# The first two weight panels of a hybrid decoder step multiplied together, k tile by k tile, with the sums of squares and the first rotation rearranged

## The chip, the cores and the metric

The kernel runs on one core of a Trainium2 chip. The metric is the device time of one execution in microseconds (us). Five engines of the core run beside each other, each taking its own instructions strictly in the order in which they were written: TensorE (matmuls; PE in the profile, PEld for its weight loads), VectorE (DVE), ScalarE (ACT), GpSimd (POOL) and SyncE (SP, which here only issues transfers). Waits between engines are by semaphores. Matmuls write to PSUM, and VectorE and ScalarE read results from there.

## What is computed

One layer of a decoder for 512 prompt tokens and 8 sample tokens together (520 columns), all float32. The stage that matters here is the beginning:

```python
u = rmsnorm(x, g_norm1)                       # x * rsqrt(mean(x^2) + eps) * g
qa, ka, va, qb, kb, vb, glr, rb, ga, gb = split(u @ w_in)
qa = rope(qa, pos); ka = rope(ka, pos)        # [x1*cos - x2*sin, x2*cos + x1*sin]
...                                           # windowed attention A, gated linear attention B, mix, MLP
```

The key buffers, value buffers and states of both groups are outputs too.

## The kernel before

**Layout.** Everything is kept transposed: 128 features on the partitions, the 520 tokens in the free dimension, as two halves of 260 columns. The model width of 1024 is eight k tiles. A *panel* is 128 output columns of a weight matrix with its eight k tiles, 512 KB. The panels are numbered in the order of use: 0 and 1 are the two halves (x1 and x2 of the rotation) of the first group's k, 2 and 3 those of its q, 4 and 5 its v, 6 and 7 the k of the second group, 8 and 9 its q, and so on to the MLP.

**A product in three passes.** To keep float32 accuracy, the activations and weights are each split into a high and a low part: `uh` and `ul` (lines 218 and 219), `whi` and `wlo` (lines 90 and 91, four k tiles at a time). ScalarE makes the high part, VectorE subtracts it from the original to get the low one. For each k tile TensorE then does high x high, low x high and high x low, each on two halves: six matmuls, so 48 for one panel (line 124). The names in the profile say which: `mps<-uh,whi`, `mps<-ul,whi`, `mps<-uh,wlo`.

**The norm comes late.** `uh` and `ul` hold x times g, not normalised. The sum of squares of each token runs beside the first panels (`stats`, line 230): eight squares on ScalarE, seven additions on VectorE, a matmul with ones that sums over the partitions (line 242), and an inverse root (`rsqrt`, lines 184 to 189) that gives `rb`. It is multiplied in later: the first pair, panels 0 and 1, is rotated with the plain cos and sin tables and scaled at the end (line 289); then `rb` is multiplied into the tables (line 848), and every later rotation comes out scaled.

**The rotation** (`rope_pair`, line 271). Panel A times cos and times sin (lines 276, 277), panel B times sin and times cos (280, 281), one subtraction and one addition of these `rt` tiles into `ro` (284, two instructions each), and eight transfers by SP that bring the result into `KTt` or `QTt` (291).

**The buffers that set the order.** Raw panels have two buffers, so the load of panel n+2 waits for the splitting of panel n. `whi` and `wlo` have four buffers each, of half a panel: the first half of panel n+2 can be split when TensorE is through the first half of panel n, the second half when TensorE is through with panel n. PSUM has two tiles for products (`pm`), and one more that panel 2 alone uses (`ps`): panel 3 takes panel 0's tile, panel 4 that of panel 1, panel 5 that of panel 3, and each has to wait until VectorE has read it.

**Who sets the order.** The kernel is written as a sequential program, and a scheduler puts each engine's instructions in an order by a model of their times; instructions written under `high_priority` go before others that are ready. `panel_mms` splits the next panel in this way (line 114). What stands in a queue when an engine waits stays behind the wait.

**The beginning** (`start`, line 197). SP issues k tile 0 of x, panel 0 in two halves, the other k tiles of x, panel 1, then the tables and panel 2. TensorE runs 20 matmuls on ones meanwhile (`keep_warm`), then panel 0, panel 1, panel 2 and so on, one after the other.

Of the kernel before, what the change touches and what calls it, by code (L numbers as in the profile page):

```python
# [21 lines left out]
P = 128  # L22
HC = 260
# [17 lines left out]
def halves(t):  # L41
    return t.rearrange("p (j c) -> p j c", j=2)


class Build:
# [24 lines left out]
    def load_panel(self, i, parts=1):  # L70
        src, kt = self.panels[i]
        raw = self.rawp.tile([P, kt, P], F32, tag="raw", name="raw", bufs=self.rawb)
        for x in range(parts):
            ks = slice(x * kt // parts, (x + 1) * kt // parts)
            self.nc.sync.dma_start(raw[:, ks], src[:, ks])
        self.raw[i] = raw

    def split_panel(self, i):

        nc = self.nc  # L80
        src, kt = self.panels[i]
        raw = self.raw.pop(i)
        self.split[i] = out = []
        for x in range(0, kt, 4):
            n = min(4, kt - x)
            if i in self.wdst:
                hi, lo = (t[:, x:x + n] for t in self.wdst[i])
            else:
                hi, lo = (self.wp.tile([P, n, P], F32R, tag=t, name=t, bufs=self.wbufs) for t in ("whi", "wlo"))
            nc.scalar.activation(hi, raw[:, x:x + n], AF.Copy)  # L90
            nc.vector.tensor_tensor(lo, raw[:, x:x + n], hi.bitcast(F32), op=ALU.subtract)  # L91
            out.append((hi, lo))
# [13 lines left out]
    def panel_mms(self, xh, xl, m, pool=None):  # L106


        nc, i = self.nc, self.cur
        self.cur += 1  # L110
        if i + 2 < len(self.panels):
            self.load_panel(i + 2)
        if i + 1 < len(self.panels):
            with self.tc.high_priority():
                self.split_panel(i + 1)
        wt = self.split.pop(i)
        kt = KT // m
        for c in range(m):
            ps = [] if c % 2 else (pool or self.pm).tile([P, 2, 512], F32, tag="m", name="mps")
            out = [self.bank("mps")[:, :HC] if c % 2 else ps[:, j, :HC] for j in range(2)]  # L120
            for k in range(kt):
                for n, (w, x) in enumerate(self.passes(wt, c * kt + k, xh, xl)):
                    for j in range(2):
                        self.last = nc.tensor.matmul(  # L124
                            out[j], w, x[:, k, j * HC:(j + 1) * HC],
                            start=(k == 0 and n == 0), stop=(k == kt - 1 and n == 2))
                self.emit_tiny(self.tiny_rate)
            yield out if c % 2 else ps[:, :, :HC]
# [68 lines left out]
    def start(self):  # L197
# [15 lines left out]
        self.keep_warm(20)  # L213
        self.eps = self.cp.tile([P, 1], F32, tag="eps", name="eps")
        nc.vector.memset(self.eps, EPS)
        nc.scalar.preload_act_table_set("natural_log_exp_and_others")
        for k in range(KT):
            self.split_x = nc.scalar.activation(self.uh[:, k], xr[:, k], AF.Copy, scale=self.g("n1", k))
            nc.vector.scalar_tensor_tensor(self.ul[:, k], xr[:, k], self.g("n1", k), self.uh[:, k].bitcast(F32),  # L219
                                           op0=ALU.mult, op1=ALU.subtract)  # L220
            if k == 0:
                self.split_panel(0)
        return xr
# [6 lines left out]
    def stats(self, ap, xr):  # L230
# [3 lines left out]
        for k in range(KT):  # L234
            a = ap.tile([P, NT], F32, tag="sq", name="sq", bufs=6)
            self.after(nc.scalar.activation(a, xr[:, k], AF.Square), self.split_x)
            if acc is None:
                acc = a
            else:
                nc.vector.tensor_tensor(acc, acc, a, op=ALU.add)  # L240
# [13 lines left out]
    def rope_tables(self):  # L254
# [5 lines left out]
        return self.cs, self.sn  # L260
# [10 lines left out]
    def rope_pair(self, dst, gi, psA, mmB, late=None):  # L271
# [4 lines left out]
        nc.vector.tensor_tensor(V[0], psA, cs, op=ALU.mult)  # L276
# [5 lines left out]
        for x, (a, b, op) in enumerate(((0, 2, ALU.subtract), (3, 1, ALU.add))):  # L282
            o = self.rp.tile([P, NT], F32, tag="ro", name="ro", bufs=3)
            self.cols(o, gi > 0, lambda ov, sel: nc.vector.tensor_tensor(ov, sel(V[a]), sel(V[b]), op=op))
            if late and x == 0:
                late()
            if late:
                rbv = halves(self.rb)
                self.cols(o, False, lambda ov, sel: nc.vector.tensor_tensor(ov, ov, sel(rbv), op=ALU.mult))
# [8 lines left out]
    def proj_qk(self, gi, late=None):  # L298
        nc, O = self.nc, self.O
        for dst, out in ((self.KTt, O["kT"]), (self.QTt, None)):  # L300
            self.rope_pair(dst, gi, self.mm(), self.mm, late)
            late = None
# [494 lines left out]
    def run(self):  # L797
# [30 lines left out]
        xr = self.start()  # L828
# [9 lines left out]
        rp, aps, gps, gss = (ExitStack() for _ in range(4))  # L838
        right = dict(bufs=1, side="right")
        self.rp = rp.enter_context(tc.tile_pool(name="rp", **right))  # L840
        with ps_stack:
            cs = self.rope_tables()

            def late():
                with tc.tile_pool(name="stp", **right) as p:
                    self.stats(p, xr)
                for t in cs:
                    nc.vector.tensor_tensor(t, t, self.rb, op=ALU.mult)

            self.late_consts()  # L850
            self.proj_qk(0, late)
# [333 lines left out]
```

## Time and profile before

| | |
|---|---|
| median of three timed runs | 938.59 us (937.89 to 943.15) |
| the profiled execution | 939.2 us |
| its span, first to last instruction | 937.4 us |
| TensorE busy | 920.3 us, 98% |
| VectorE busy | 549.0 us, 59% |
| ScalarE busy | 380.0 us, 41% |
| TensorE's mean granted clock | 0.993 |
| moved by DMA | 155.27 MB, 166 GB/s on average |

Busy time is the time in which an engine has an instruction in work; matmuls overlap, so 98% doesn't say that TensorE does as much as it could, only that it is seldom without work. Times in a profile count from the first instruction. In a timeline a row has the start, the time, the engine, the line of the kernel, the operation, the tile written and those read, the shape, and in brackets how long the engine had been idle before it and for whom it waited. The granted clock is the share of full speed at which TensorE was allowed to run.

### The profile page before, as it was taken

The numbers are of one execution on the slowest core, as the hardware profiler recorded it, in microseconds if no ns is written. First come the engines' busy times: TensorE is split into PE (matmuls) and PEld (weight loads), VectorE is DVE, ScalarE is ACT, GpSimd is POOL, SyncE is SP. The second block draws the span as 40 slices with busy tenths as digits, with TensorE's granted clock in tenths as the row PEclk, the third lists the DMA queues.
The fourth block names the chain that finished last, engine by engine and source line by source line (L and its number), as shares of the span: only waits on it lengthen the run. The fifth ranks groups of instructions, "written<-read, shape, count | busy, mean of one in ns | idle before, by whom it ended". The sixth has DMA issues, their size and how long they took to land.

```text
span 937.4 us, 19831 instructions
## 1 busy us (share of the span) xinstructions
PE 920.3 (98%) x8306; PEld 896.3 (96%) x8306; DVE 549.0 (59%) x1078; ACT 380.0 (41%) x735; POOL 67.4 (7%) x119
## 2 busy tenths in 40 slices
PE   9899999999999999999999999999999999999995
PEld 9899999999998999989999999999999999999995
DVE  7757566665766949586855556433443345555654
ACT  6133423443645536565633443322432243224432
POOL 1000000000201112010000000010000000000000
PEclk9899999999999999999999999999999999999998
DMA  6365454233444444222677767777865232323301
GB/s 245 114 237 181 142 191 155 101 131 116 166 150 165 128 165 144 69 74 69 235 278 277 272 226 269 270 269 270 294 254 175 96 93 87 104 92 106 121 30 63
DMA packets 37147, 155.27 MB, mean 166 GB/s; under 512 B 5129, under 2 KB 11537, under 8 KB 35106
## 3 DMA queue, kind: packets, MB, share of 16 engines
q1 hardware_dynamic: 32066, 95.26, 29.8%
q0 software_dynamic: 4848, 58.73, 18.0%
q8 instruction: 65, 1.06, 0.5%
q14 instruction: 24, 0.20, 0.1%
q10 hardware_dynamic: 144, 0.01, 0.0%
HBM read 140.66 MB, written 54.17 MB: 208 GB/s over the span
## 4 chain that ended last, share of the span: by engine, by line
PE 95%; DVE 2%; DMA 1%; issue 1%; ACT 0%; SPq 0%; DVEq 0%; ACTq 0%
PE mps L124 80%; PE mps L1017 5%; PE pvp L383 1%; PE lev L583 1%; PE gpo L670 1%; PE vps L318 1%; PE ptp L368 1%; PE gpu L674 1%; PE sps L352 1%; DMA xr<-in_xT 1%; PE gso L737 1%; PE gpo L672 1%; PE sps L347 1%; PE mps L547 0%; PE zp L592 0%
## 5 line engine op out<-in xcount | busy, mean ns | idle before, releaser
L90 ACT ACTIVATE whi<-raw 128x512 fp32r<-128x512 f32 x264 | 165.7, 630 | 358.6 <-PE mps L124 325.6
L91 DVE TENSOR_TENSOR wlo<-raw,whi 128x512 fp32r<-128x512 f32 x264 | 183.4, 695 | 152.2 <-ACT whi L90 149.9
L124 PE MATMUL mps<-uh,whi 128*128 128x260 f32 x928 | 194.0, 288 | 3.0 <-DVE rt L281 3.0
L124 PE MATMUL mps<-ul,whi 128*128 128x260 f32 x928 | 194.3, 288 | 0.2 <-DVE ul L219 0.2
L124 PE MATMUL mps<-uh,wlo 128*128 128x260 f32 x928 | 191.5, 286 | 0.0
L124 PEld LDWEIGHTS mps<-uh,whi 128*128 128x128 f32 x928 | 144.6, 190 | 6.1 <-issue 5.5
L124 PEld LDWEIGHTS mps<-ul,whi 128*128 128x128 f32 x928 | 145.2, 190 | 3.1 <-issue 1.7
L124 PEld LDWEIGHTS mps<-uh,wlo 128*128 128x128 f32 x928 | 144.7, 189 | 1.2 <-issue 0.8
L124 PE MATMUL mps<-hh,wlo 128*128 128x260 f32 x512 | 103.2, 283 | 0.0
L124 PE MATMUL mps<-hh,whi 128*128 128x260 f32 x512 | 103.2, 283 | 0.0
L124 PE MATMUL mps<-hl,whi 128*128 128x260 f32 x512 | 103.0, 283 | 0.0
L124 PEld LDWEIGHTS mps<-hh,whi 128*128 128x128 f32 x512 | 79.0, 188 | 0.1
L124 PEld LDWEIGHTS mps<-hh,wlo 128*128 128x128 f32 x512 | 79.0, 188 | 0.0
L124 PEld LDWEIGHTS mps<-hl,whi 128*128 128x128 f32 x512 | 78.7, 188 | 0.0
L124 PE MATMUL mps<-fh,wlo 128*128 128x260 f32 x384 | 77.3, 283 | 0.0
L124 PE MATMUL mps<-fl,whi 128*128 128x260 f32 x384 | 77.2, 283 | 0.0
L124 PE MATMUL mps<-fh,whi 128*128 128x260 f32 x384 | 76.8, 282 | 0.0
L124 PEld LDWEIGHTS mps<-fh,wlo 128*128 128x128 f32 x384 | 59.2, 188 | 0.0
L124 PEld LDWEIGHTS mps<-fl,whi 128*128 128x128 f32 x384 | 59.0, 188 | 0.0
L124 PEld LDWEIGHTS mps<-fh,whi 128*128 128x128 f32 x384 | 59.0, 188 | 0.0
L1017 PE MATMUL mps<-fh,lw 128*128 128x260 f32 x256 | 46.6, 283 | 0.0
L1017 PEld LDWEIGHTS mps<-fh,lw 128*128 128x128 f32 x256 | 39.6, 188 | 0.1
(336 smaller groups left out, 1301.1 us busy)
## 6 DMA issues: line engine op xcount, KB each, us to landing
raw<-in_w_in SPq DMA_DIRECT2D x57, 512.0 KB, 3.3
raw<-in_w_up SPq DMA_DIRECT2D x32, 512.0 KB, 4.0
raw<-in_w_down SPq DMA_DIRECT2D x32, 512.0 KB, 5.2
sx<-in_state SPq DMA_DIRECT2D x8, 512.0 KB, 4.9
sx<-dV SPq DMA_DIRECT2D x8, 512.0 KB, 4.7
out_sgla<-sx POOLq DMA_DIRECT2D x8, 512.0 KB, 5.7
raw<-in_w_pb SPq DMA_DIRECT2D x8, 512.0 KB, 5.5
raw<-in_w_o SPq DMA_DIRECT2D x8, 512.0 KB, 5.5
```

Of the source, the lines that this page charges most:

```text
L90: nc.scalar.activation(hi, raw[:, x:x + n], AF.Copy)
L91: nc.vector.tensor_tensor(lo, raw[:, x:x + n], hi.bitcast(F32), op=ALU.subtract)
L124: self.last = nc.tensor.matmul(out[j], w, x[:, k, j * HC:(j + 1) * HC], start=(k == 0 and n == 0), stop=(k == kt - 1 and n == 2))
L318: nc.tensor.transpose(pt[:, r * P:(r + 1) * P], vt[:, r * P:(r + 1) * P], self.c["ident"])
L347: nc.tensor.matmul(pss[hh][:, hp, first * P:], Q[rows, hp, b * P:(b + 1) * P], K[rows, hp, (b - 1 + first) * P:(b + 1) * P], start=True, s ...
L352: nc.tensor.matmul(pss[hh][:, hp, gg * P:(gg + 1) * P], Q[rows, i, b * P:(b + 1) * P], K[rows, i, b * P:(b + 1) * P], start=True, stop=True)
L368: nc.tensor.transpose(pt[:, hh, x], prs[hp][:, hh, x * P:(x + 1) * P], self.c["ident"])
L383: nc.tensor.matmul(po[64 * hh:64 * hh + 64, hp * P:(hp + 1) * P], v, pTs[hp][:, hh, x], start=(x == first), stop=(x == 1))
L583: self.nc.tensor.matmul(ps[32 * i:32 * i + 32, c], k[:, 32 * b:32 * b + 32], q[:, n * b:n * b + n], start=True, stop=True)
L670: nc.tensor.matmul(po[:, :256], ST[:, c], V[:, c], start=True, stop=(c == 0))
L672: nc.tensor.matmul(po[:, :256], qe[:, c * P:(c + 1) * P], st, start=False, stop=True)
L1017: nc.tensor.matmul(ps, w, x[:, kk, cc], start=(kk == 0 and n == 0), stop=(kk == KT - 1 and n == 2))
```

## The change

The first two panels are multiplied together. Their raw weights come in four pieces of four k tiles, in the order panel 0 and panel 1, and the pieces of x come between them. For each k tile, `uh` and `ul` are made, and then the six matmuls of panel 0 and the six of panel 1 are written (`k_tile`), into two PSUM tiles at once. The two tiles are both of `pm`, as before. After the loop come the load of panel 2, the tables, the load of panel 3, and the splitting of panel 2.

The warm-up has 10 matmuls instead of 20. `stats` is written right behind `start` and wholly at high priority; before, it was written inside the first rotation. The first rotation is told to wait for the last addition of the squares (`self.added`). As before, the first pair alone is rotated with plain tables and then scaled; the scaling now follows in program order for both `ro` tiles, and the tables are multiplied by `rb` after the pair rather than within it.

```diff
-    def load_panel(self, i, parts=1):
...
+    def load_panel(self, i):
+        self.raw[i] = self.raw_tile(i)
+        self.nc.sync.dma_start(self.raw[i], self.panels[i][0])
+
+    def raw_tile(self, i):
+        return self.rawp.tile([P, self.panels[i][1], P], F32, tag="raw", name="raw", bufs=self.rawb)
+
+    def split_piece(self, raw, x, n, dst=None):
+        nc = self.nc
+        hi, lo = dst or (self.wp.tile([P, n, P], F32R, tag=t, name=t, bufs=self.wbufs) for t in ("whi", "wlo"))
+        nc.scalar.activation(hi, raw[:, x:x + n], AF.Copy)
+        nc.vector.tensor_tensor(lo, raw[:, x:x + n], hi.bitcast(F32), op=ALU.subtract)
+        return hi, lo
...
+    def k_tile(self, out, w, kw, k, xh, xl, kt):
+
+        for n, (wt, x) in enumerate(self.passes(w, kw, xh, xl)):
+            for j in range(2):
+                o = out[j] if isinstance(out, list) else out[:, j]
+                self.last = self.nc.tensor.matmul(o[:, :HC], wt, x[:, k, j * HC:(j + 1) * HC],
+                                                  start=(k == 0 and n == 0), stop=(k == kt - 1 and n == 2))
...
+        raw = [self.raw_tile(i) for i in range(2)]
+
+        def weights(x):
+            for i in range(2):
+                nc.sync.dma_start(raw[i][:, x:x + 4], self.panels[i][0][:, x:x + 4])
+
         nc.sync.dma_start(xr[:, 0], I["xT"][:, 0])
-        self.load_panel(0, 2)
-        for a, b in ((1, 2), (2, 4), (4, 6), (6, 8)):
-            nc.sync.dma_start(xr[:, a:b], I["xT"][:, a:b])
-        self.load_panel(1)
+        weights(0)
+        nc.sync.dma_start(xr[:, 1], I["xT"][:, 1])
+        nc.sync.dma_start(xr[:, 2:4], I["xT"][:, 2:4])
+        weights(4)
+        for a in (4, 6):
+            nc.sync.dma_start(xr[:, a:a + 2], I["xT"][:, a:a + 2])
...
-        self.keep_warm(20)
+        self.keep_warm(10)
...
+        ps = [self.pm.tile([P, 2, 512], F32, tag="m", name="mps") for _ in range(2)]
+        w = [[], []]
         for k in range(KT):
             self.split_x = nc.scalar.activation(self.uh[:, k], xr[:, k], AF.Copy, scale=self.g("n1", k))
...
-            if k == 0:
-                self.split_panel(0)
-        return xr
+            for i in range(2):
+                if k % 4 == 0:
+                    w[i].append(self.split_piece(raw[i], k, 4))
+                self.k_tile(ps[i], w[i], k, k, self.uh, self.ul, KT)
+        self.cur = 2
+        self.load_panel(2)
+        self.rope_tables()
+        self.load_panel(3)
+        with self.tc.high_priority():
+            self.split_panel(2)
+        return xr, [p[:, :, :HC] for p in ps]
...
-        nc.vector.tensor_tensor(V[0], psA, cs, op=ALU.mult)
+        r = nc.vector.tensor_tensor(V[0], psA, cs, op=ALU.mult)
+        if rb is not None:
+            self.after(r, self.added)
...
-            if late and x == 0:
-                late()
-            if late:
-                rbv = halves(self.rb)
-                self.cols(o, False, lambda ov, sel: nc.vector.tensor_tensor(ov, ov, sel(rbv), op=ALU.mult))
+            if rb is not None:
+                self.cols(o, False, lambda ov, sel: nc.vector.tensor_tensor(ov, ov, sel(halves(rb)), op=ALU.mult))
...
+            if first:
+                self.rope_pair(dst, gi, first[0], lambda: first[1], self.rb)
+                for t in (self.cs, self.sn):
+                    nc.vector.tensor_tensor(t, t, self.rb, op=ALU.mult)
+                first = None
+            else:
+                self.rope_pair(dst, gi, self.mm(), self.mm)
...
-            cs = self.rope_tables()
-
-            def late():
-                with tc.tile_pool(name="stp", **right) as p:
-                    self.stats(p, xr)
-                for t in cs:
-                    nc.vector.tensor_tensor(t, t, self.rb, op=ALU.mult)
-
+            with tc.tile_pool(name="stp", **right) as p, tc.high_priority():
+                self.stats(p, xr)
             self.late_consts()
-            self.proj_qk(0, late)
+            self.proj_qk(0, first)
```

**TensorE at the beginning.** Before, behind the warm-up (numbers tell buffers apart: `mps_177` is panel 0's product, `whi_118` and `wlo_119` its first weights; each row is the two halves of one pass):

```order
L124 MATMUL mps_177<-uh_76,whi_118 128x260 x2
L124 MATMUL mps_177<-ul_77,whi_118 128x260 x2
L124 MATMUL mps_177<-uh_76,wlo_119 128x260 x2
L124 MATMUL mps_177<-uh_76,whi_118 128x260 x2
L124 MATMUL mps_177<-ul_77,whi_118 128x260 x2
L124 MATMUL mps_177<-uh_76,wlo_119 128x260 x2
L124 MATMUL mps_177<-uh_76,whi_118 128x260 x2
L124 MATMUL mps_177<-ul_77,whi_118 128x260 x2
```

These are k tiles 0 and 1, and the first two passes of k tile 2; ahead of its low part stand seven rows, 14 matmuls. After the change, at the same place (`mps_110` is panel 0, `mps_111` panel 1; `whi_114` and `wlo_115` are panel 0's first weights, `whi_124` and `wlo_125` panel 1's):

```order
L129 MATMUL mps_110<-uh_79,whi_114 128x260 x2
L129 MATMUL mps_110<-ul_80,whi_114 128x260 x2
L129 MATMUL mps_111<-uh_79,whi_124 128x260 x2
L129 MATMUL mps_111<-ul_80,whi_124 128x260 x2
L129 MATMUL mps_110<-uh_79,wlo_115 128x260 x2
L129 MATMUL mps_110<-uh_79,whi_114 128x260 x2
L129 MATMUL mps_111<-uh_79,wlo_125 128x260 x2
L129 MATMUL mps_111<-uh_79,whi_124 128x260 x2
L129 MATMUL mps_110<-ul_80,whi_114 128x260 x2
L129 MATMUL mps_110<-uh_79,wlo_115 128x260 x2
L129 MATMUL mps_111<-ul_80,whi_124 128x260 x2
L129 MATMUL mps_111<-uh_79,wlo_125 128x260 x2
```

These twelve rows are k tiles 0 and 1 of both panels; the high parts of k tile 2 for both follow, and then its low part. Ahead of that low part now stand 28 matmuls instead of 14. The sum over the partitions (`rps<-sq,ones`) moves too: it stood behind 182 panel matmuls, 38 into panel 3, and now stands behind 144, between panels 2 and 3. From panel 8 on, TensorE's order is that of before.

**VectorE ahead of panel 5.** Before, from the end of `rsqrt` to the second rotation (`ro_293` and `ro_342` are the first pair's results, `wlo_569` panel 6's first low part, `mps_362` and `mps_427` the products of panels 2 and 3):

```order
L189 SCALAR_TENSOR_TENSOR rb_324<-ra_326,rb_324 128x520
L848 TENSOR_TENSOR cs_149<-cs_149,rb_324 128x520
L91 TENSOR_TENSOR wlo_569<-raw_496,whi_568 128x512
L848 TENSOR_TENSOR sn_150<-sn_150,rb_324 128x520
L289 TENSOR_TENSOR ro_293<-ro_293,rb_324 128x512
L289 TENSOR_TENSOR ro_293<-ro_293,rb_324 128x8
L289 TENSOR_TENSOR ro_342<-ro_342,rb_324 128x512
L289 TENSOR_TENSOR ro_342<-ro_342,rb_324 128x8
L276 TENSOR_TENSOR rt_411<-mps_362,cs_149 128x520
L277 TENSOR_TENSOR rt_412<-mps_362,sn_150 128x520
L280 TENSOR_TENSOR rt_413<-mps_427,sn_150 128x520
L281 TENSOR_TENSOR rt_414<-mps_427,cs_149 128x520
```

After the change, the twelve rows that end at the same place (`wlo_494` is panel 5's second low part, `wlo_560` panel 6's first; `ro_322` and `ro_331` are the first pair, `mps_353` and `mps_418` panels 2 and 3); `rb` is made in the row ahead of them:

```order
L81 TENSOR_TENSOR wlo_494<-raw_408,whi_493 128x512
L308 TENSOR_TENSOR ro_322<-ro_322,rb_290 128x512
L308 TENSOR_TENSOR ro_322<-ro_322,rb_290 128x8
L308 TENSOR_TENSOR ro_331<-ro_331,rb_290 128x512
L308 TENSOR_TENSOR ro_331<-ro_331,rb_290 128x8
L323 TENSOR_TENSOR cs_242<-cs_242,rb_290 128x520
L323 TENSOR_TENSOR sn_243<-sn_243,rb_290 128x520
L81 TENSOR_TENSOR wlo_560<-raw_487,whi_559 128x512
L296 TENSOR_TENSOR rt_402<-mps_353,cs_242 128x520
L299 TENSOR_TENSOR rt_403<-mps_353,sn_243 128x520
L302 TENSOR_TENSOR rt_404<-mps_418,sn_243 128x520
L303 TENSOR_TENSOR rt_405<-mps_418,cs_242 128x520
```

The scaling of the first pair now stands ahead of that of the tables, and panel 5's second low part stands ahead of both; it was split ahead of `rsqrt`'s last two steps before. Both queues end with the four products that read panel 2 and panel 3 out of PSUM.

**SP behind the loads of the first panels.** Before (`raw_566` is panel 7, `raw_640` panel 8; `KTt` and `QTt` take the rotated k and q of the first group):

```order
L75 DMA raw_566<-in_w_in 128x1024
L291 DMA KTt_143<-ro_293 32x520 x4
L291 DMA KTt_143<-ro_342 32x520 x4
L291 DMA QTt_144<-ro_478 32x520 x4
L291 DMA QTt_144<-ro_485 32x520 x4
L75 DMA raw_640<-in_w_in 128x1024
```

After (`raw_557` is panel 7, `raw_631` panel 8):

```order
L72 DMA raw_557<-in_w_in 128x1024
L310 DMA KTt_259<-ro_322 32x520 x4
L310 DMA KTt_259<-ro_331 32x520 x4
L72 DMA raw_631<-in_w_in 128x1024
L310 DMA QTt_260<-ro_469 32x520 x4
L310 DMA QTt_260<-ro_476 32x520 x4
```

Panel 8's load has moved from behind the eight transfers of q to ahead of them.

More of the change, by code (lines that the diff above doesn't have):

```diff
@@ L67, in bank @@
         return self.pf.tile([P, 512], F32, tag="f", name=name)
-    def load_panel(self, i, parts=1):
[L71 to L76, printed above, removed]
+    def load_panel(self, i):
[9 more added lines that the diff above has]
+        return hi, lo
     def split_panel(self, i):
-        nc = self.nc
         src, kt = self.panels[i]
         raw = self.raw.pop(i)
[L83 to L92, printed above, removed]
+        self.split[i] = [self.split_piece(raw, x, min(4, kt - x),
+                                          i in self.wdst and [t[:, x:x + min(4, kt - x)] for t in self.wdst[i]])
+                         for x in range(0, kt, 4)]
     def passes(self, w, k, xh, xl):
```

27 lines of the change are left out of this document (10 added, 17 removed).

## The prediction

> **What bounds the kernel now.** I read the page first: what share of the span TensorE is busy, who stands in the chain that ended last, and what clock it was granted.
>
> ```profile
> span 937.4 us, 19831 instructions
> ...
> PEclk9899999999999999999999999999999999999998
> ...
> PE 95%; DVE 2%; DMA 1%; issue 1%; ACT 0%; SPq 0%; DVEq 0%; ACTq 0%
> ```
>
> TensorE carries 95% of the chain. The work it has to do is the same after the change but for ten warm-up matmuls, so only its idle time and its clock can move the end. In the clock line the second of forty slices (23 to 47 us) is below the rest (the last holds the end, where TensorE has finished). Next, the waits of TensorE over the whole span (total us, times, longest):
>
> ```profile
> PE mps L124 <- DVE rt L281: 3.0, 1, 3.0
> PE vps L318 <- DVE vt L310: 1.1, 1, 1.1
> ```
>
> There is little to win, and the largest piece lies in the change's stage: one wait of 3.0 us on the rotation. The windows around it give busy time, granted clock and DMA:
>
> ```profile
> 38.00:39.00 1.00, 0.46 (x4) 1.00 0.00 0
> ...
> 40.00:41.00 1.00, 0.00 (x0) 0.73 0.51 123
> 41.00:42.00 1.00, 0.54 (x2) 0.50 0.32 77
> ...
> 47.00:48.00 1.00, 1.00 (x9) 0.85 1.01 404
> ```
>
> TensorE stops at 38.46. The mean of 0.73 in the microsecond from 40 means that the clock fell to 0.50 at 40.46, 2.0 us into the wait; the 0.85 from 47 means that it came back at 47.3. The wait costs twice: idle, and half speed behind it. The chain of waits in order of time (start, us, what) prices both:
>
> ```profile
> 36.23 0.69 DVE wlo L91
> 36.92 0.61 DVE sn L848
> 37.53 1.36 DVE ro L289 x4
> 38.89 0.61 DVE rt L276
> ...
> 40.71 0.62 DVE rt L281
> 41.33 0.14 issue
> 41.46 4.67 PE mps L124 x20
> 46.13 0.85 PE vps L318 x4
> 46.98 6.80 PE mps L124 x55
> 53.78 0.44 PE vps L318 x4
> 54.22 2.51 PE mps L124 x21
> 56.73 0.65 PE sps L347 x8
> 57.38 0.31 PE sq L448 x2
> 57.69 5.77 PE mps L124 x48
> ```
>
> Panel 5 starts at 41.46. From there to 57.69 TensorE does 96 panel matmuls, 8 transposes and the scores, in 16.23 us. At full clock a panel of 48 takes 5.77 us (last row), four transposes 0.44: 2 x 5.77 + 2 x 0.44 + 0.65 + 0.31 = 13.38. The low clock costs **2.85 us**.
>
> **The start.** The timeline by engine:
>
> ```profile
> 1.05 7.23 PE L228 MATMUL rps<-ones 128*128 128x128 f32 x40 [1.05 <-DVE eps L215]
> ...
> 4.41 0.63 ACT L90 ACTIVATE whi<-raw 128x512 fp32r<-128x512 f32 x1
> ...
> 5.96 0.63 ACT L90 ACTIVATE whi<-raw 128x512 fp32r<-128x512 f32 x1 [0.91 <-DMA raw<-in_w_in]
> 6.60 0.73 ACT L218 ACTIVATE uh<-xr,gcols 128x520 fp32r<-128x520 f32 x1
> ...
> 8.61 3.97 ACT L218 ACTIVATE uh<-xr,gcols 128x520 fp32r<-128x520 f32 x6 [1.27 <-DMA xr<-in_xT]
> ...
> 9.37 4.12 DVE L219 SCALAR_TENSOR_TENSOR ul<-xr,gcols,uh 128x520 fp32r<-128x520 f32 x6 [1.24 <-ACT uh L218]
> ...
> 10.19 0.51 PE L124 MATMUL mps<-ul,whi 128*128 128x260 f32 x2 [0.21 <-DVE ul L219]
> ...
> 14.19 2.74 ACT L236 ACTIVATE sq<-xr 128x520 f32<-128x520 f32 x5
> ```
>
> The warm-up runs to 8.28, though the first weights are split at 5.0. At 10.19 TensorE waits for the low part of k tile 2. By the order of instructions it has then issued 14 matmuls of panel 0.
>
> Five transfers lead SP's queue up to k tiles 2 and 3, and the change keeps their sizes and order (260, 256, 256, 260, 520 KB); only the third is now panel 1's first half instead of panel 0's second. So I take k tile 2 as ready at 10.19 again. By then the new order has issued 28 matmuls, 14 for each panel. Do they fit? Ten warm-up calls are half of the 40 hardware matmuls: half of 7.23 us gives 4.7, and as the early ones are the slower (421 against 275 ns, in a row further down) I take 5.3; the inputs are later anyway. Four matmuls follow, then panel 1's weights (loaded at 5.96, split at 6.59), k tile 1 (its low part near 8.1) and the rest, all done by 9.84: yes. Both versions then run without a gap, so the change is ahead by 14 matmuls:
>
> ```profile
> 10.19 20.43 PE mps L124 x168
> 30.62 0.89 PE rps L242 x4
> ```
>
> 20.43 / 168 = 0.1216 us each. Panels 0 and 1 end at 10.19 + 82 x 0.1216 = 20.16 now, at 10.19 + 68 x 0.1216 = 18.46 then: **1.70 us** earlier.
>
> That needs the later k tiles in time. ScalarE and VectorE now split both second halves of the weights before k tile 4, two more conversions of 0.63 us: the last high part ends at 12.58 + 1.26 = 13.84 instead of 12.58, and the low part of k tile 4 near 12.7 (k tile 4: 8.61 + 2 x 0.66 + 1.26 + 0.73 + 0.76; TensorE asks for it at 10.19 + 24 x 0.1216 = 13.1). The last transfer of activations moves behind 512 KB of weights; now it is there by 11.25 (the fifth of the six in the row), and it may come some 2 us later before TensorE, which reaches k tile 6 at 15.5, notices.
>
> Then panel 2. Its conversion stands behind six squares on ScalarE: 13.84 + 6 x 0.55 = 17.1, converted at 17.8. On VectorE its low part stands behind four additions,
>
> ```profile
> 16.40 1.50 DVE L240 TENSOR_TENSOR sq<-sq 128x520 f32<-128x520 f32 x2
> ```
>
> 0.75 us each: from 14.95 to 17.95, then 0.69 for the low part, 18.64. TensorE asks for it four matmuls into panel 2, at 18.95. Covered, by only 0.3 us; if that cover goes, it costs what is missing. Behind the fourth addition stand four low parts and three more additions, 4 x 0.69 + 3 x 0.75 = 5.0: the seventh ends at 22.95, and the sum over partitions is due at 18.46 + 5.84 = 24.3. The first rotation's new wait on this addition holds VectorE's queue; due first behind it are panel 0's two products, which must leave PSUM before panel 3 starts at 24.3 + 0.89 = 25.2 and end at 22.95 + 2 x 0.7 = 24.35. Covered by 0.8 us.
>
> **The wait before panel 5.** It needs panel 3's PSUM tile, which the second rotation frees. Now the sum over partitions stands 38 matmuls into panel 3, then ahead of panel 3: 4.6 us earlier in the program. So rsqrt no longer ends last. What does? VectorE's queue holds the low part of panel 5's second half ahead of the final scaling, and that needs panel 3's buffers:
>
> ```profile
> 25.86 0.63 ACT L90 ACTIVATE whi<-raw 128x512 fp32r<-128x512 f32 x1 [2.24 <-PE mps L124]
> ...
> 26.52 0.69 DVE L91 TENSOR_TENSOR wlo<-raw,whi 128x512 fp32r<-128x512 f32 x1 [0.45 <-ACT whi L90]
> ```
>
> Here it starts 0.14 before its panel's end (20.16 + 48 x 0.1216 = 26.0), and VectorE follows at +0.52. TensorE's end of panel 4 comes 1.70 earlier, at 38.46 - 1.70 = 36.76, so panel 3 ends at 36.76 - 5.84 = 30.92 and this subtraction starts at 31.44. Behind it the chain of the rows above (subtraction, sn, four ro, four rt: 36.23 to 41.33, 5.10 us), plus the cos table (0.61, as sn) and panel 6's subtraction (0.69), which now stand in it too: 6.40. It ends at 37.84, and with the 0.14 of issue panel 5 starts at 37.98. TensorE idles **1.22 us** instead of 3.00: 1.78 gained. The clock should not fall: the listed wait of 1.1 us (vps) lies in slices whose clock stays at 9 tenths or more, and this fall came only 2.0 us into its wait. So the 2.85 goes too.
>
> The Trainium skill's page "TensorE: Matmul & The Clock Gate", section "Why this matters for your kernels", allows idle gaps up to about 3 us before the clock halves; by it 1.2 us would leave a margin of 1.8. The trace does not agree: 2.0 us of idle were enough here, so the margin is 0.8, and a fall keeps a chance of its own below.
>
> **Sum.** 1.70 + 1.78 + 2.85 = 6.33 us. Behind panel 7 the order on TensorE is the same, and no wait there is tied to a fixed time.
>
> **What moves on SP.** Panel 8's load (512 KB) now stands ahead of the eight transfers of rotated q, which the first scores need:
>
> ```profile
> 43.36 5.19 SPq L291 DMA_DIRECT2D QTt<-ro  x8
> ...
> 54.06 0.23 DVE L442 TENSOR_TENSOR qd<-QTt,qmask 128x64 f32<-128x64 f32 x1 [2.03 <-DMA QTt<-ro]
> ...
> 55.95 1.20 ACT L90 ACTIVATE whi<-raw 128x512 fp32r<-128x512 f32 x2 [1.10 <-DMA raw<-in_w_in]
> ```
>
> First issue to last landing is 10.7 us. After the change the first follows rt's end as now (41.33 to 43.36): 37.84 + 2.03 = 39.87, the last landing is at 50.6. TensorE reaches the scores at 56.73 - 6.33 + three matmuls (0.36) = 50.76. Today's reserve of 2.7 us is gone. The price lies between 0 and, with the load wholly in front, that load's time: 512 KB took 7.4 us there (issued when q's row ends, 48.55, there at 55.95). I take 0, the nearest row being q's own 10.7, and keep the rest for the range. POOL's constant loads start 1.3 us later, with the last k tile, and nothing here waits for them.
>
> **The forecast.** The profiled execution took 939.2 us (span 937.4); 939.2 - 6.33 = 932.9. The median of the three timed runs, 938.59, is 0.6 lower: **932.3 us**. A measurement of this kernel can tell about 0.5%, 4.7 us, from no change; the forecast is 0.67%.
>
> **Rivals.** *The clock.* The early window
>
> ```profile
> L228 PE MATMUL rps<-ones x9: 275/275/421, 5.7 to 6.9; 128*128 128x128 f32 x9
> ```
>
> shows matmuls going from 421 to 275 ns after TensorE had been busy since 1.05, so about 6.3. With half the warm-up and gaps for inputs between 6 and 10 us, the rise could slip; by half of the low spell seen here (40.46 to 47.3, 6.84 us) it costs 3.4 / 2 = 1.7. Or the 1.2 us wait makes the clock fall after all, 2.85. Times: 934.0 and 935.2. For it: TensorE idles in both places. Against: the gaps are under 0.4 us each, the 1.1 us wait did no harm. The Trainium skill speaks against halving the warm-up: "TensorE: Matmul & The Clock Gate", Part 1, wants a busy window of about 3.4 us, and the window runs freely, so 4.25 us of calls need not fill one. By that rule the rise may come one window later, at the same 1.7 us; the trace's own rise, 5.3 us after the first matmul, agrees with it, and that is in the chance.
>
> *It doesn't run as the inputs arrive.* If the weights that now stand ahead hold back the last k tiles by over 4 us, panels 0 and 1 end no earlier: 1.70 is lost, the rest stays, 934.0. For it: 512 KB more ahead of them. Against: the queue is as long in sum, and TensorE is the slower of the two from k tile 3.
>
> *Slower: q's transfers.* If panel 8's load goes wholly ahead of them and takes its 7.4 us, q lands at 58.0, TensorE waits 7.2 us at the scores, the clock falls again (2.85): 932.3 + 10.05 = 942.4. It turns into a loss once q lands 3.5 us late (3.5 + 2.85 = 6.35), and is over 0.5% from 8.2 on. For it: q and that load share a queue, and the key cache's 1 MB comes at the same time. Against: the load is issued before q's issue even begins, and q's issue alone takes 5.2 us. A mild form, 1 to 1.7 us late with the clock kept, gives 933.3 to 934.
>
> **How the numbers follow.** Forecast 0.52 (931 to 933.5 alone); q mildly late 0.12; clock 0.17; inputs late 0.13; q very late 0.06, half of it beyond 0.5%. Faster by over 0.5% is below 933.9: forecast, most of mildly late and a little of clock and inputs, 0.64; within, 0.33; slower, 0.03. The range goes from 930.5 (panel 5's wait gone too, 1.2, and some spread) to 937 (clock and q late together).
>
> **What would show it.** TensorE's first panel matmul near 5.3; panels 0 and 1 ended near 18.5; the sum over partitions near 24.3 to 25.2; one wait of about 1.2 us on rt before panel 5 near 38 and no clock under 1.00 between 7 and 900 us; no wait of sps on q. Wrong would be: a wait on wlo at panel 2, a clock of 0.50 anywhere after 7 us, a wait at sps, or a new wait behind panel 8.

## The result, and the profile after

The changed kernel takes **933.79 us** (median of eight runs, 932.67 to 937.03) against 938.66 before: a ratio of **0.9941, with a 95% interval of 0.9923 to 0.9958**; the medians are 4.9 us apart. The ratio comes from all of these runs and need not be the quotient of the medians. The profiled execution took 933.32 us, 5.88 less than that of before. Its page:

```profile
span 931.5 us, 19801 instructions
...
PEclk9999999999999999999999999999999999999998
...
PE 95%; DVE 2%; DMA 1%; issue 0%; ACT 0%; SPq 0%; DVEq 0%; ACTq 0%
```

TensorE still carries 95% of the chain; the dip in the second slice of the clock line is gone. The waits of TensorE (total us, times, longest), where 3.0 stood before:

```profile
PE mps L129 <- DVE rt L303: 1.1, 1, 1.1
PE vps L342 <- DVE vt L334: 1.1, 1, 1.1
```

The chain of waits in order of time (start, us, what), around the places that the prediction names:

```profile
18.09 0.70 DVE wlo L81
18.83 5.54 PE mps L129 x44
24.37 0.88 PE rps L262 x4
...
33.51 0.61 DVE cs L323
34.12 0.61 DVE sn L323
34.73 0.60 DVE wlo L81
35.33 0.61 DVE rt L296
...
37.16 0.62 DVE rt L303
37.77 0.14 issue
37.91 3.00 PE mps L129 x23
40.91 0.44 PE vps L342 x4
41.34 6.24 PE mps L129 x52
47.58 0.44 PE vps L342 x4
48.02 2.89 PE mps L129 x24
50.91 1.09 PE sps L371 x8
...
52.31 5.42 PE mps L129 x45
```

Panel 5 starts at 37.91 instead of 41.46, 3.55 us sooner. TensorE is through panel 7 (384 panel matmuls) at 52.31 + 5.42 = 57.73 instead of 57.69 + 5.77 = 63.46: **5.73 us** sooner, which is nearly the whole 5.9 by which the span is shorter. Two rows are worse than forecast: TensorE waits some 0.2 us for panel 2's low part (made from 18.09 to 18.79), and the eight matmuls of the scores (`sps`) take 1.09 us, where they took 0.65 before.

### The profile page after: what moved, and what is told of

Same layout as the page of the kernel before. It is cut to its first block, busy times and chain, and to the rows that moved or that the text cites. A ratio compares the mean times of both kernels' runs of the same rounds, so it can differ in the third digit from the quotient of the medians.

```text
span 931.5 us, 19801 instructions
## 1 busy us (share of the span) xinstructions
PE 916.4 (98%) x8286; PEld 891.9 (96%) x8286; DVE 549.5 (59%) x1078; ACT 380.5 (41%) x735; POOL 66.2 (7%) x119
## 4 chain that ended last, share of the span: by engine, by line
PE 95%; DVE 2%; DMA 1%; issue 0%; ACT 0%; SPq 0%; DVEq 0%; ACTq 0%
PE mps L129 80%; PE mps L1035 5%; PE pvp L407 1%; PE lev L607 1%; PE gpo L694 1%; DMA xr<-in_xT 1%; PE ptp L392 1%; PE gpu L698 1%; PE vps L342 1%; PE sps L376 1%; PE gso L761 1%; PE gpo L696 1%; PE sps L371 1%; PE mps L571 0%; PE zp L616 0%
```

## The experiments

Timed runs of this kernel scatter by more than some of the effects, so the table has beside the times a number of the profile that says what happened in the changed stage alone: when TensorE was through panel 7, read from the chain as above (the end of its row, within 0.01 the start of the row that follows, `ptp`). Each of these numbers comes from one profiled execution.

| kernel | through panel 7, us | sooner than before | profiled run | median (runs) | ratio to before, 95% interval |
|---|---|---|---|---|---|
| before | 63.46 | | 939.2 | 938.66 (8) | |
| the change | 57.73 | 5.73 | 933.32 | 933.79 (8) | 0.9941 [0.9923, 0.9958] |
| the change again | 57.94 | 5.52 | 933.49 | 933.48 (5) | 0.9946 [0.9934, 0.9958] |
| statistics alone | 57.74 | 5.72 | 933.39 | 933.93 (6) | 0.9952 [0.9939, 0.9965] |
| pairing alone | 64.03 | -0.57 | 939.57 | 938.75 (12) | 1.0000 [0.9989, 1.0011] |
| busy wait | 61.27 | 2.19 | 936.92 | 937.25 (11) | 0.9988 [0.9980, 0.9997] |
| before, ten warm-up calls | 64.46 | -1.00 | 940.16 | 940.42 (12) | 1.0009 [0.9998, 1.0021] |
| change, twenty warm-up calls | 59.28 | 4.18 | 934.80 | 934.72 (9) | 0.9963 [0.9951, 0.9976] |
| change, q first | 57.25 | 6.21 | 932.79 | 932.79 (5) | 0.9947 [0.9934, 0.9960] |
| change, low part later | 57.77 | 5.69 | 933.35 | 932.56 (5) | 0.9941 [0.9928, 0.9954] |
| change, three orders moved | 56.05 | 7.41 | 934.19 | 933.95 (6) | 0.9929 [0.9912, 0.9946] |
| statistics alone, key cache later | 58.33 | 5.13 | 936.70 | 934.20 (6) | 0.9939 [0.9922, 0.9957] |
| three orders, `kl` on VectorE | 56.16 | 7.30 | 931.26 | 931.60 (4) | 0.9908 [0.9889, 0.9927] |
| before, `kl` on VectorE | 63.44 | 0.02 | 938.50 | 937.72 (12) | 0.9977 [0.9965, 0.9990] |

The kernel before ran beside each of the five groups of runs, with medians of 938.66, 938.57, 938.23, 940.23 and 940.08; each ratio is against the one beside it.

**1. The statistics alone.** The squares and their sum written behind panel 0's matmuls, scaling and tables as in the change (`first` calls `stats` at high priority):

```diff
-            self.rope_pair(dst, gi, self.mm(), self.mm, late)
+                psA = self.mm()
+                first()
+                self.rope_pair(dst, gi, psA, self.mm, self.rb)
+                for t in (self.cs, self.sn):
+                    nc.vector.tensor_tensor(t, t, self.rb, op=ALU.mult)
```

> The kernel before with the statistics' half of the change alone: squares and sum over partitions at high priority behind panel 0's matmuls (the sum 140 matmuls in instead of 182), the raw rotation for the first pair, the final scaling as in the change; panels 0 and 1 one after the other as before, twenty warm-up calls. Here panel 5's second low part stands behind the final scaling on VectorE, straight ahead of the second rotation's products. Theory (the wait before panel 5 is set by what stands behind that low part): it starts 0.5 us after panel 3's end (32.6 + 0.5), the chain behind it is 0.69 + 4 x 0.61 = 3.1 us and ends near 36.3, ahead of panel 4's end at 38.46; so no wait before panel 5, no fall of the clock, gain 3.0 + 2.85 = 5.85 us, as much as the whole change although the first term (1.70) is missing. Rival (the terms add as forecast): gain 1.78 + 2.85 = 4.6 us with a wait of about 1.2 us left.

57.74: this half alone is as fast as the whole change. Its timeline on VectorE:

```profile
33.55 0.69 DVE L305 TENSOR_TENSOR sn<-sn,rb 128x520 f32<-128x520 f32 x1
34.16 0.68 DVE L91 TENSOR_TENSOR wlo<-raw,whi 128x512 fp32r<-128x512 f32 x1
34.77 0.69 DVE L276 TENSOR_TENSOR rt<-mps,cs 128x520 f32<-128x520 f32 x1
...
36.59 0.68 DVE L283 TENSOR_TENSOR rt<-mps,cs 128x520 f32<-128x520 f32 x1
```

The `wlo` row is panel 5's second low part. It stands behind the scaled tables, and panel 3 ends (near 32.6) while VectorE is still scaling, so VectorE never waits for that end. The four products are done at 37.3, before TensorE is through panel 4 (100 of the 141 matmuls in the row from 26.41 below, at 0.12 us each: 38.4). The chain has no step between the sum over partitions and the first V transposes:

```profile
25.54 0.88 PE rps L242 x4
26.41 16.93 PE mps L124 x141
43.34 0.44 PE vps L324 x4
```

No wait before panel 5, no fall of the clock, as expected.

**2. The pairing alone.** Loads, ten warm-up calls and the k tile order of the change, with `stats` inside the first rotation as before.

> The kernel before with the other half alone: panels 0 and 1 together, k tile by k tile, loads and ten warm-up calls as in the change; squares, sum and scaling where they were before, inside the first rotation (the sum 180 matmuls in). Theory: panels 0 and 1 end 1.7 us earlier, but the last two steps of rsqrt, both tables, the scaled halves and panel 6's low part stand behind panel 5's second low part, so the wait before panel 5 stays near 3 us (2.6 to 3.3) and the clock falls again; gain 1.7 to 2.1 us. Rival (the clock depends on where the wait falls and not only on its length): the wait stays, the clock does not fall, gain 4.5 to 5 us. Rival (the pairing is hidden behind the rotation): gain 0.

```profile
PE mps L129 <- DVE rt L301: 2.8, 1, 2.8
PE mps L129 <- ACT whi L80: 1.3, 2, 0.9
...
PE sps L370 <- DMA QTt<-ro: 0.8, 2, 0.5
```

No gain, the size of the third outcome, by another way than any of the three. The wait before panel 5 is there as expected (2.8), and this time the clock did not fall behind it, so its length alone doesn't decide. Waits on high parts, the longest 0.86 at panel 2, left 0.37 of the pairing's lead at panel 5 (41.09). TensorE then came to the scores before q, and behind that wait the clock did fall: the panel that follows took 7.29 us in the chain instead of 5.77.

**3. A busy wait.** Behind panel 4:

```diff
-            vt = self.scaled(self.mm(), "vt", nt >= 2)
+            ps = self.mm()
+            if nt == 0:
+                for _ in range(13):
+                    nc.tensor.matmul(self.mps[:, 0, 384:384 + P], self.ones, self.ones, start=True, stop=True)
+            vt = self.scaled(ps, "vt", nt >= 2)
```

> The kernel before with 13 matmuls of ones on ones added behind panel 4, into columns of its PSUM tile that nothing reads: TensorE is busy for most of the 3.0 us in which it otherwise waits for the second rotation. No work is removed. Theory (the low clock behind the wait is a price of its own, 2.85 us, caused by the idle time): panel 5 starts when it did, near 41.5, the clock stays at 1.00, gain 2.85 us (2 to 3), with 13 matmuls more than before. Rival (the fall has nothing to do with idle TensorE): clock falls as before, gain 0 or a loss of up to 1 us from the first V scaling starting later.

```profile
38.07 2.92 PE mps L328 x26
40.98 0.08 issue
41.07 3.60 PE mps L124 x28
...
53.71 0.42 PE sps L352 x4
...
54.21 0.46 PE sps L352 x2
...
54.70 0.48 PE sps L352 x2
```

(Each of the 13 matmuls is two in the profile, as in the warm-up.) The clock stayed up, in all eleven runs at a mean of 0.996 or 0.997, and the kernel got faster although it does 13 matmuls more: idle TensorE had lowered the clock. From panel 5's start to the end of panel 7 it takes 61.27 - 41.07 = 20.20 us instead of 63.46 - 41.46 = 22.00; of that the scores now take 1.48 instead of 0.65. So the low clock costs 1.80 + 0.83 = 2.63 us, and 0.83 of it is lost again because TensorE now reaches the scores before q does.

**4. Before, with ten warm-up calls.**

```diff
-        self.keep_warm(20)
+        self.keep_warm(10)
```

> The kernel before with ten warm-up calls instead of twenty and nothing else. Theory of the prediction (the inputs, not the warm-up, set the start: k tile 2 is ready at 10.19): panels 0 and 1 end where they did, gain 0 (within 0.3 us); the clock rises near 6 us as in both kernels. Rival (the warm-up itself held the start back, and the pairing did little): gain near 1.7 us. Rival (half the warm-up lets the clock rise one window later): loss of about 1.7 us.

In the stage 1.0 us slower, towards the third of these, though in another form; the ratio of the times, 1.0009 with an interval from 0.9998 to 1.0021, does not tell it from no change. The windows (from:to, their length, busy time of TensorE and matmuls, clock, DMA share, GB/s):

```profile
7.00:8.00 1.00, 0.21 (x1) 1.00 0.99 366
8.00:9.00 1.00, 0.71 (x5) 1.00 1.00 395
9.00:10.00 1.00, 0.80 (x6) 0.66 1.02 394
...
12.00:13.00 1.00, 1.00 (x7) 0.63 1.08 426
...
57.00:58.00 1.00, 1.00 (x7) 0.56 0.00 0
```

The clock had come up at 6, but TensorE had too little to do behind the ten calls, and it fell again from 9.32 to 12.74 (as the means of 0.66 and 0.63 say). At the sum over partitions this cost little (30.87 instead of 30.62). The larger part came later: this run's wait before panel 5 left the clock up, TensorE waited 1.0 us for q at the scores, and the clock fell behind them. In the changed kernel panel 1's matmuls fill the early gap; its shorter warm-up belongs to the pairing.

**5. The change again, and with twenty warm-up calls.**

> The changed kernel itself, for the comparison with the three that follow and for a second profile at another phase of the clock. Expected: 933.3 to 934.0 us median; one wait of 1.0 to 1.3 us on the rotation before panel 5, the scores 0.2 to 0.6 us longer than 0.65. Theory (the 1.1 us wait now and then lets the clock fall, by the phase): a few of the runs lie 2 us above the others, with a mean clock lower by 0.002; rival (the wait is too short for that): all runs within 1.5 us.

> The changed kernel with twenty warm-up calls as before instead of ten. Its first panel matmul then comes near 8.3 instead of 5.35 us, 2.9 us later, and TensorE has inputs enough not to idle behind it. Theory (the pairing's earlier start is mostly given back at the wait before panel 5 and at the scores, which the rotation and q's transfers set): the 14 matmuls done before k tile 2 (1.7 us) are the most that the late start can cost; the wait before panel 5 is bound by panel 3's end and stays near 1.1; loss 1.2 to 1.9 us, so 935.0 to 935.7. Rival (the late start is hidden at that wait): loss under 0.5 us. Rival (ten calls cost clock in some runs, as in the kernel before with ten): the fastest runs slower by 1.5 us, but the slowest runs gone, the median about the same.

The change again: 932.68 to 933.95, the same 1.1 us wait, no fall in the profile, and all runs within 1.3 us, as the rival has it. What made the two runs of the first eight above 935 (at mean clocks of 0.994 and 0.995) isn't shown: it may be the cause of experiment 8, and five runs do not rule out a fall behind this wait now and then. Twenty calls: 1.3 us later in the stage than this, 1.2 in the median, as expected, but not by the expected way: the first panel matmul came at 8.29, and the scheduler then put panel 5's second low part behind the scaled tables, so there was no wait before panel 5 at all, and 1.3 us at the scores instead.

**6. q first, and the low part later.** Two orders without a wait, each in a kernel of its own: panel 8's load behind the last transfer of q (`moved`), and panel 5's second low part behind the second rotation's last product:

```diff
+        if i == 8:
+            self.behind(ld, self.moved)
...
+        if i == 5:
+            self.behind(self.low, self.products)
```

> The changed kernel with panel 8's load put behind the eight transfers of rotated q on SP's queue by an order without a wait. Theory (the scores' 0.44 us are a wait for q's transfers, which that load delays): q's last landing comes 1.2 us or more sooner, the 8 matmuls of the scores take 0.65 to 0.7 again, the wait before panel 5 stays 1.1; gain over the changed kernel 0.4 to 0.5 us. Rival (q lands late because its transfers themselves are slow beside the key cache, not because of that load): scores as before, gain 0. Rival (panel 8's load is then itself late): a new wait at panel 8.

```profile
50.53 0.65 PE sps L378 x8
```

The scores take 0.65 again, 0.48 us of the stage are gained. In SP's timeline q's eight transfers are issued in 5.48 us (second row) instead of the 6.43 of the change (first row):

```profile
39.74 6.43 SPq L310 DMA_DIRECT2D QTt<-ro  x8
...
39.72 5.48 SPq L317 DMA_DIRECT2D QTt<-ro  x8
```

> The changed kernel with panel 5's second low part put behind the second rotation's products on VectorE by an order without a wait (panel 6's first low part follows it, and on SP panel 7's load goes behind rotated k's transfers, panel 8's behind q's). Theory (this low part, which waits for panel 3's end, and the chain behind it are the whole wait before panel 5): final scaling and tables run from 30.7 us on, the four products need only panel 3's end at 30.9, the chain ends near 35.8, ahead of panel 4's end at 36.8; no wait before panel 5, none at the scores; gain over the changed kernel 1.1 + 0.4 = 1.5 us, 932.2 us median, and no run with a fallen clock. Rival (the next thing is late at once: panel 5's second half, panel 6 or 7, or q at the scores): the wait moves and the gain is under 0.5 us.

The wait before panel 5 is gone, as expected, but one of 1.1 us stands at the scores, so in the stage nothing is won: the rival. SP's timeline of this run shows why:

```profile
36.44 0.53 SPq L72 DMA_DIRECT2D raw<-in_w_in  x1
37.52 7.81 SPq L317 DMA_DIRECT2D QTt<-ro  x8
```

Panel 7's load, which needs the raw buffer that the postponed low part frees, now runs beside q's transfers, and beside the 1 MB of key cache; q's issue takes 7.81 us. It started 2.2 us sooner and ended only 0.8 us sooner (45.33 instead of 46.17).

**7. Three orders moved.** Panel 5's second low part behind the tables (as in experiment 1), panel 8's load behind q, and the first group's key cache load (`ld`) after the first use of q on VectorE (`q`); and this last order for the statistics alone:

```diff
+            if gi == 0:
+                self.after(ld, q)
```

> The changed kernel with three orders moved, no work less: panel 5's second low part behind the scaled tables and panel 6's first low part behind the second rotation's products on VectorE (as the statistics' half alone had them); panel 8's load behind rotated q's transfers; the first group's 1 MB of key cache on POOL's queue only after q has landed. Theory (the pairing's 1.7 us at the start is there, and was given back at the wait before panel 5, 1.1, and at the scores, 0.4, where q's transfers share the DMA engines with 1 MB of key cache and a 512 KB panel): no wait before panel 5, the scores in 0.65 to 0.7, panel 8 starts 1.5 us sooner than in the changed kernel, near 56.2; 931.9 to 932.4 us median. Rival (q's transfers are slow whatever runs beside them): the wait moves to the scores as in the run before, panel 8 near 57.7, no gain. Rival: the key cache comes too late for VectorE's products (needed near 63), a new wait behind panel 9.

> The statistics' half alone, panels 0 and 1 one after the other and twenty warm-up calls, with the same key cache order: the counterpart of the run beside it without the pairing. Theory (with both waits gone the path is TensorE's own work from its start on, and the pairing is worth its 14 matmuls): scores 0.65, gain 0.2 us over the statistics' half before, panel 8 near 57.5, and 1.3 to 1.7 us slower than the run beside it. Rival (the pairing is worth nothing even then): the two within 0.5 us.

The chain of the first:

```profile
25.36 14.91 PE mps L135 x124
...
49.32 0.65 PE sps L382 x8
...
50.28 5.77 PE mps L135 x48
```

No wait is left behind panel 2, and TensorE is through panel 7 at 56.05: 1.68 us sooner than the change, 1.69 sooner than the statistics alone. About 0.2 of the latter is the scores (0.65 instead of 0.84); the rest, 1.5, is the pairing: its 14 matmuls (14 x 0.1216 = 1.70) less 0.2 that TensorE still waits for panel 2's low part. The second run agrees: it is 2.27 behind, and its inputs came 0.76 later than those of experiment 1 (its chain reaches k tile 2 at 10.91 instead of 10.15), which leaves 1.5. The median landing of q's transfers came down to 2.7 us in the first run, from 6.9 in the change and 5.5 with q first. But the times fell short of the expectation, for a reason far behind the stage. The list of waits of the first:

```profile
PE klp L650 <- POOL kl L647: 2.9, 1, 2.9
```

This wait was 0.6 us in both kernels; in both runs of this pair it was 2.9, and the clock fell for 3.4 us behind it. `kl` is a product that GpSimd makes for the gated attention near 410 us. Of the six timed runs of the first kernel two took 931.21 and 931.47, with a mean clock of 0.997, and four 933.85 to 934.21 at 0.994 to 0.995.

**8. `kl` on VectorE.**

```diff
-        nc.gpsimd.tensor_tensor(kl, kl, k, op=ALU.mult)
+        nc.vector.tensor_tensor(kl, kl, k, op=ALU.mult)
```

> The changed kernel with the three moved orders of the run before last, and the gate's four products of decay and key (128x512, exp on ScalarE, product, transposes on TensorE) on VectorE instead of GpSimd. Theory (runs of one kernel differ by 2 to 3 us because this product on GpSimd, beside VectorE's products from the same tile near 409 us, takes 1.6 us in some executions and 3.9 in others, and in the latter TensorE waits 2.9 instead of 0.6 and the clock falls): on VectorE it takes 0.7, no wait of 0.6 or 2.9 on it, all runs within 1 us of each other near 930.5 to 931.5, mean clock 0.996 to 0.997. Rival (the scatter has another cause, the clock's phase at the start): still two groups 2 to 3 us apart. Rival (the scheduler's other order, which the edit brings, costs as much): one group, but at 932 or more.

> The kernel before with only those four products on VectorE. Theory: the group of runs above 940 goes, the rest stays, 937 to 938; the run beside it is then faster by the change's gain and the 1.5 us of the moved orders, 6 to 7 us in all. Rival: as before, with two groups.

With it the runs draw together: the first takes 931.26 to 931.92 in all four, at a clock of 0.997, and beats both kernels (0.9908); the kernel before takes 937.18 to 939.25, where on the same chip it took 937.83 to 942.95 as it was. So most of the scatter was this product. The two medians lie 6.1 us apart, at the low end of what was expected; the first kernel's 931.6 is 0.1 above its range. No run has the statistics alone with `kl` on VectorE, so what the pairing is worth is shown in the stage, not in the medians.

## Why the prediction was right or wrong

The forecast was 932.3 us, in a range of 930.5 to 937; the result is 933.79. Two of the signs that were to mean a wrong forecast did come, both small: a wait on `wlo` at panel 2 and a wait at the scores.

**The start: right.** The first panel matmul came at 5.35 (forecast 5.3), panel 2's first at 18.13 (18.46), the sum over partitions at 24.37 to 25.24 (24.3 to 25.2). k tile 2 was even 0.9 us earlier than taken.

**The cover at panel 2: too thin.** It was given as 0.3 us. The low part ended at 18.79 (18.64), TensorE would have asked at about 18.6, and some 0.2 us were lost.

**The wait before panel 5: right, cause and size.** 1.13 us (1.22), panel 5 from 37.91 (37.98). That panel 5's second low part and the chain behind it set it was shown by experiments 1, 6 and 7: wherever that low part stood behind the tables or behind the products, the wait was gone.

**The clock: right in the profile, too large for the median.** It did not fall. Experiment 3 measures the term at 2.63 instead of 2.85 us. But the profiled execution of before was one with a full fall of two windows, and not all are: in the kernel before with `kl` on VectorE, where little else scatters, the two runs with a mean clock of 0.997 took 937.18 and 937.47, the profiled one, with a fall of 6.8 us at a mean of 0.993, 938.5. And keeping the clock up is worth 2.19 us in the stage but 1.3 in the medians of experiment 3. The step that was off is the last, from 932.9 for a profiled execution to a median 0.6 lower: the profiled change took 933.32, and the medians of its two groups, 933.79 and 933.48, are not below that. A likely reason is that those 0.6 were part of the fall, which was counted as gone already; with one trace of each kernel this isn't shown.

**q's transfers: the term taken as 0 was 0.44.** The mild form of the rival came true. Experiment 6 shows that panel 8's load, moved ahead of q, was the cause. It and the 0.2 more that TensorE took from panel 5's start to the scores than by the rows of before (13.00 instead of 12.78; the cause is open) are the difference between 6.33 and 5.73. The heavy form did not come: q was issued in 6.4 us in spite of the load ahead.

**What the sum did not show.** 1.70 was credited to the pairing. In this change the pairing gained nothing: the statistics alone are as fast (57.74 against 57.73). Both kernels lose the old wait and the fall. With the sum over partitions and 144 panel matmuls done, the change leads the statistics alone by 1.7 us (25.24 against 26.41 + 4 x 0.12 = 26.9). This lead is given back as 1.13 before panel 5, some 0.2 from there to the scores and 0.25 at the scores (1.09 against 0.84), since the scheduler then put the low part ahead of the tables and panel 8's load ahead of q. So that the total of 5.73 came near 6.33 doesn't bear out the 1.70 as the pairing's gain. Experiment 7, with those two orders and the key cache moved, keeps the lead: 1.5 us.

## What to carry to other kernels

A lead at the start is worth only what the next fixed point lets through: after moving work, look for what sets the next two waits, and which instructions the scheduler has put between. Apply each half of a change alone; here one half carried the gain, and the other one paid, in the stage, once the orders behind it were mended. When timed runs scatter, compare the stage in the profile, and look for a stretch whose duration differs between two profiles of the same work.

## What the runs showed of the hardware

**The clock changes on a grid.** In the kernel before it fell at 40.46 and rose at 47.3, 6.84 us later. In experiment 4's windows above it falls at 9.32, rises at 12.74 and falls at 57.12 (0.56 in the microsecond from 57): the distances are 3.42 and 44.38, that is 1 and 13 times 3.414, and 6.84 is twice 3.42. So where a wait lies on this grid, whose phase differs between runs, may decide whether it brings a fall: 3.0 us of waiting with 2.0 of them in one step made the clock fall, 2.8 us in experiment 2, with 1.6 in one step and 1.2 in the next (counted back from its rise at 60.4), did not. But it isn't the idle time alone: waits of 0.8 and 1.0 us at the scores were followed by a fall in experiments 2 and 4, those of 1.3 and 1.1 us there in experiments 5 (twenty calls) and 6 (low part later) were not, nor was the wait of 1.1 us before panel 5 in any of three profiles. What TensorE must do in a step to keep its clock stays open. The Trainium skill, "TensorE: Matmul & The Clock Gate", Part 1, gives a free-running window of 3413 ns; these rows agree with it. They do not agree with the section "Why this matters for your kernels" of that page of the Trainium skill, which allows idle gaps up to about 3 us.

**GpSimd and VectorE block each other.** The product `kl` and VectorE's products from the same tile in the timeline of the changed kernel:

```profile
409.93 0.69 DVE L81 TENSOR_TENSOR wlo<-raw,whi 128x512 fp32r<-128x512 f32 x1
410.14 1.62 POOL L634 TENSOR_TENSOR kl<-kl,QKb 128x512 f32<-128x512 f32 x1 [16.95 <-ACT kl L633]
410.54 1.50 DVE L652 TENSOR_TENSOR D<-D,QKb 128x256 f32<-128x256 f32 x1
...
413.39 0.41 DVE L669 TENSOR_TENSOR D<-D,QKb 128x256 f32<-128x256 f32 x1
```

and of the kernel with three orders moved:

```profile
408.20 0.69 DVE L83 TENSOR_TENSOR wlo<-raw,whi 128x512 fp32r<-128x512 f32 x1
408.41 3.88 POOL L647 TENSOR_TENSOR kl<-kl,QKb 128x512 f32<-128x512 f32 x1 [16.95 <-ACT kl L646]
408.80 0.42 DVE L665 TENSOR_TENSOR D<-D,QKb 128x256 f32<-128x256 f32 x1
...
410.48 0.69 DVE L83 TENSOR_TENSOR wlo<-raw,whi 128x512 fp32r<-128x512 f32 x1
```

The same rows in the same order, begun 0.2 and 0.4 us apart in both. In the first GpSimd goes through (1.62) and VectorE's product takes 1.50 instead of 0.41; in the second VectorE's run through at 0.42 and GpSimd's takes 3.88, to 1.1 us behind the end of the last of them. Ten of the profiles up to experiment 7 show the first form, the two of experiment 7 the second, which costs TensorE 2.3 us of waiting and a fall of the clock. That the two engines exclude each other for whole instructions agrees with the Trainium skill, "SBUF — State Buffer", section "SBUF: two separate sides", by which a VectorE instruction with two inputs in SBUF and a GpSimd one that reads SBUF share ports under an exclusive lock that goes to whoever starts first. Which of them gets it here, with the same start in both, no run shows.
